# Tile homes moved to 96 bytes above a multiple of 128, and another order at the end of layer 0's output projection

## The chip, the cores and the metric

The kernel runs on one core of a Trainium2 chip. The metric is the time of one execution on the device in microseconds (us). The runs of the kernel before took 1118.15, 1120.03 and 1122.57 us; their median is 1120.03 us. The profile is of a further execution, which took 1121.99 us.

## The reference, cut to what matters

The program is a decoder trunk of two layers on 512 tokens of width 1024, all in float32. Each layer adds a mixer and then a SwiGLU feed-forward part to the residual stream.

```python
for layer in range(2):
    h = h + mixer(rms_norm(h, g), w_in, ..., w_out)      # even_mixer, then odd_mixer
    h = h + swiglu(rms_norm(h, ffn_g[layer]), w_gate, w_up, w_down)
return rms_norm(h, final_norm_g)

def even_mixer(h, w_in, sinks, conv_w, conv_b, ln_g, ln_b, w_out, pos):   # layer 0
    q, k, v, glu = split(h @ w_in)
    a = band_attention(rotary(q), rotary(k), v, 127, sinks)   # 8 heads, 2 key heads, window 128
    c = glu_a * sigmoid(glu_b)
    c = silu(layer_norm(causal_depthwise_conv(c, conv_w, conv_b), ln_g, ln_b))   # width 31
    return concat([a, c]) @ w_out
```

Layer 0's output projection reads eight tiles of 128 channels: four of attention, four of the convolution. Layer 1 mixes a dilated attention with a gated product; its arithmetic is not touched.

## The kernel before, in words

**Products.** Activations lie transposed: a tile has 128 channels as partitions and 512 tokens along them. A float32 product is done as three products of a faster type: each operand is split into a high part (ScalarE rounds it) and a low part (VectorE or GpSimd subtracts), and `acc3` (L197 on) multiplies high by high, high by low and low by high (L201 to L203), each a matmul of 512 columns. In the projections the weights (`w_hi`, `w_lo`) are the stationary operand and the activation streams. In the feed-forward part the first two products are done in seven block products (L909, L911, L912), where the weights (`w2h`, `w2l`) stream and the activations are stationary: `xh`, `xl` in three of the seven, sums `s1` to `s4` in four. The down product is again `acc3`, with the hidden tiles `hh`, `hl` streaming.

**Homes.** Every tile has a fixed address in each partition, handed out in the order of the calls, each rounded up to 32 bytes. The pools `const`, `keep`, `wpool` and `scr` stand for the whole kernel; a fourth region is used in turn by the pools of layer 0's mixer, of the feed-forward part and of layer 1's mixer. The build gives these homes (address modulo 512, and modulo 128):

| tiles | mod 512 | mod 128 |
|---|---|---|
| `ident` | 288 | 32 |
| `h`, `xh`, `xl`, `raw`, `w_hi`, `w_lo` | 352 | 96 |
| feed-forward: `w2h`, `w2l`, `raw2`, `hh`, `hl`, `s1` to `s4` | 288 | 32 |
| layer 1's mixer: `oh`, `ol`, `st` | 288 | 32 |
| layer 0's mixer: `oh`, `ol`, `yc`, `khh`, `qs` | 416 | 32 |

**Order.** TensorE runs its instructions in the order in which they are written out. A planner in the kernel (`Seq`) writes it: it keeps a clock of its own, adds 0.682 us for each `acc3` and lets generators step in when their due times have come: scores (`scores0`), values (`values0`, which calls `pt_av`) and the convolution's layer norm (`conv_norm`). The due times are the constants of `C0`. `until` jumps the clock to the next due time when a step needs a result that the plan has not reached. The other engines are ordered by the framework, each engine in order again.

In layer 0, `pt_av` transposes the softmax tiles in groups of four (L407), ScalarE copies each group out of PSUM (`pts`, L410), and TensorE multiplies it by the values (L421); VectorE normalises (`on`, L430), and TensorE transposes back (L435). `at[g]` is the planned time from which a group may be multiplied: 0.9 us after its transposes (`TA`).

The convolution runs beside this: `conv_tile` has 31 taps for each of four channel tiles, some on ScalarE with GpSimd (L478, L479), most on VectorE (L481, L483), and a last sum (L484). `conv_norm` transposes each finished channel tile (L645), gathers statistics (L647), and after the fourth forms the norm and transposes back (L672); a SiLU on ScalarE (L675) and a split give the tiles `L0` to `L3` that the projection needs.

The word list `steps` orders all this. `A0` to `A3` are the projection of attention tile 0 to 3 into the output tiles `na` = (0, 1), `X` the same into `nx` = (2, 3, 4), `Y` the four attention tiles into output 5, 6 or 7, and `B` one convolution tile into outputs 0 to 4. `C12` ends the list: for each of the outputs 0 to 4 the convolution tiles 1 and 2, and then the residual sum. Outputs 5 to 7 follow. The output tile `n` is summed in PSUM bank `n`; the last projection before `A0` (`q3`) has its result in bank 0, and `b3` had its own in bank 1.

Of the kernel before, what the change touches and what calls it, by code (L numbers as in the profile page):

```python
# [10 lines left out]
def _warn_once_fixed(msg, *args, **kwargs):  # L11
# [7 lines left out]
F32 = mybir.dt.float32  # L19
F32R = mybir.dt.float32r  # L20
AF = mybir.ActivationFunctionType
ALU = mybir.AluOpType

P = 128
S = 512
# [9 lines left out]
C0 = dict(  # L35

    first='a0 b0',
    steps='L g0 k q0 v S0 g1 q1 V0 S1 g2 q2 V1 S2 g3 q3 V2 S3 V3 A0 A1 A2 Y5 X0 X1 A3 Y6 X3 X2 Y7 B0 B3 C12',  # L40
    na=(0, 1), nx=(2, 3, 4),
    rope_v=('k', 'q2', 'q3'),
    taps=(8, 15, 15, 10),

    norm=(0.0, 2.6), q=(11.0, 7.0, 7.0, 6.0), v=1.2, S=3.13, ST=3.0, TA=0.9, AO=2.4, LB=4.85, LO=2.1, LS=3.5, ln=(60.0, 84.0, 112.0, 124.0),

    n1=5, q1=6.6, S1=2.26, ST1=3.65, m1=11.78, M1=0.53, TA1=1.12, AO1=1.4,
)
# [86 lines left out]
def trunk_kernel(ctx: ExitStack, tc: tile.TileContext, xT, ws, cols, sinks, sgu_g, sgu_b,  # L135
                 spat_wT, spat_b, rope_c, rope_s, ident_d, mask0_d, mask1_d, fin_g, y):
    nc = tc.nc
    V, A, G, T = nc.vector, nc.scalar, nc.gpsimd, nc.tensor
    ctx.enter_context(tc.manual_schedule(engines={mybir.EngineType.PE}))

    const = ctx.enter_context(tc.tile_pool(name="const", bufs=1))
    keep = ctx.enter_context(tc.tile_pool(name="keep", bufs=1))
    wpool = ctx.enter_context(tc.tile_pool(name="wpool", bufs=4))
    scr = ctx.enter_context(tc.tile_pool(name="scr", bufs=2))
    psum = ctx.enter_context(tc.tile_pool(name="psum", bufs=1, space=bass.MemoryType.PSUM))

    def bank(i, shape=None):
        return psum.tile(shape or [P, S], F32, name=f"bank{i}")
# [94 lines left out]
    seq = Seq()  # L243
# [47 lines left out]
    for k in range(2, KT):  # L291
        nc.sync.dma_start(h[k], xT[k])
        if k in (3, 6):
            dma_block()
    ident = const.tile([P, P], F32, name="ident")
    nc.sync.dma_start(ident, ident_d)
    ones = const.tile([P, 1], F32, name="ones")
    V.memset(ones, 1.0)
    mhalf = const.tile([P, 4], F32, name="mhalf")
    V.memset(mhalf, -0.5)  # L300

    idle = scr.tile([P, 256], F32, name="sq", bufs=1)
    V.memset(idle, 0.0)
# [10 lines left out]
    norm = {}  # L314
# [80 lines left out]
    def pt_av(items, vap, rl, dst, banks, line="V", ta="TA", ao="AO"):  # L395

        po = bank(5, [P, 8, 64])
        turn = [0]

        def tbank():  # L400
            turn[0] += 1
            return bank(banks[(turn[0] - 1) % len(banks)])

        def trans(grp):
            pt = tbank()
            for x, (u, pap, blk, first, last) in enumerate(grp):
                T.transpose(pt[:, x * P:(x + 1) * P], pap, ident)  # L407
            pts = mpool[0].tile([P, S], F32, name="pts", bufs=3)
            w = len(grp) * P
            A.activation(pts[:, :w], pt[:, :w], AF.Copy)  # L410
            return pts

        grps = [items[c:c + 4] for c in range(0, len(items), 4)]
        pts, at = {}, {}
        for g in range(min(2, len(grps))):
            pts[g] = trans(grps[g])
            at[g] = seq.t + 0.43 + C0[ta]
            yield 0.43, (0.0 if g == 0 else max(0.0, at[0] - seq.t - 0.43))
        for g, grp in enumerate(grps):
            for x, (u, pap, blk, first, last) in enumerate(grp):  # L420
                T.matmul(po[:, u, :], pts[g][:, x * P:(x + 1) * P], vap(u, blk), start=first, stop=last)  # L421
            cost = 0.43
            if g + 2 < len(grps):
                pts[g + 2] = trans(grps[g + 2])
                at[g + 2] = seq.t + 0.86 + C0[ta]
                cost = 0.86
            if g + 1 < len(grps):
                yield cost, max(0.0, at[g + 1] - seq.t - cost)
        on = mpool[0].tile([P, NQ, P], F32, name="on", bufs=1)
        V.tensor_mul(on.rearrange("p n (b e) -> p (n b) e", b=2), po,  # L430
                     rl[:, :, None].to_broadcast([P, 8, 64]))
        yield 0.43, C0[ao]
        pt = tbank()
        for n in range(NQ):
            T.transpose(pt[:, n * P:(n + 1) * P], on[:, n, :], ident)  # L435
        split(pt, oh_[0][dst], ol_[0][dst])
        done.add((line, dst))
        yield 0.43, 0.0
# [5 lines left out]
    with ExitStack() as mx:  # L444
        mp = mx.enter_context(tc.tile_pool(name="mix0", bufs=1))
# [5 lines left out]
        nc.sync.dma_start(sinkb, bass.AP(tensor=sinks.tensor, offset=sinks.offset, ap=[[0, P], [1, 8]]))  # L451
        nsink = mp.tile([P, 8], F32, name="nsink")
        V.tensor_scalar(out=nsink, in0=sinkb, scalar1=-1.0, scalar2=None, op0=ALU.mult)
        cp = [mp.tile([P, TAPS - 1 + S], F32, name=f"cp{j}") for j in range(4)]
        for j in range(4):
            G.memset(cp[j][:, 0:TAPS - 1], 0.0)
# [2 lines left out]
        V.tensor_scalar(out=taps, in0=taps, scalar1=0.5, scalar2=None, op0=ALU.mult)  # L459


        mp.tile([P, 8, 2 * P + 1], F32, name="Pm", bufs=2)
        for b in range(2):
            mp.tile([P, S], F32R, name=f"qs{b}", bufs=2)
        yc = [mp.tile([P, S], F32, name=f"yc{j}") for j in range(4)]
# [107 lines left out]
        def scores0(i):  # L573
            yield 0.0, C0["q"][i]
            while i >= 2 and ("V", i - 2) not in done:
                yield 0.0, 0.3
            qss = qTs[i]

            Pm = mp.tile([P, 8, 2 * P + 1], F32, name="Pm", bufs=2)
            A.activation(Pm[:, :, 2 * P:].rearrange("p (n b) o -> p n (b o)", b=2),  # L580
                         nsink[:, i:i + 5:4][:, None, :].to_broadcast([P, NQ, 2]), AF.Copy)
            nm = scr.tile([P, 8], F32, name="nm")
            l = scr.tile([P, 8], F32, name="l")
            for n2 in range(2):
                sb = [bank(2), bank(3)]
                for n1 in range(2):
                    n = 2 * n2 + n1
                    for b in range(2):
                        lo = max(n - 1, 0) * P
                        w = (n + 1) * P - lo  # L590
                        out = sb[b][:, n1 * 256 + 256 - w:n1 * 256 + 256]
                        q = slice(n * P, (n + 1) * P)
                        T.matmul(out, qss[b][:, q], khh[b][:, lo:lo + w], start=True, stop=False)
                        T.matmul(out, qss[b][:, q], kl[b][:, lo:lo + w], start=False, stop=True)
                for n1 in range(2):
                    n = 2 * n2 + n1
                    for b in range(2):
                        u = 2 * n + b
                        c0 = P if n == 0 else 0
                        hd = i + 4 * b  # L600
                        V.tensor_tensor_reduce(
                            out=Pm[:, u, c0:2 * P], in0=sb[b][:, n1 * 256 + c0:n1 * 256 + 256],
                            in1=mask0[:, c0:], scale=-0.125, scalar=nsink[:, hd:hd + 1],
                            op0=ALU.add, op1=ALU.min, accum_out=nm[:, u:u + 1])
                if n2 == 0:
                    yield 0.9, C0["S"]
            for u in range(8):
                c0 = P if u < 2 else 0
                A.activation(Pm[:, u, c0:], Pm[:, u, c0:], AF.Exp, bias=nm[:, u:u + 1], scale=-1.0,
                             accum_out=l[:, u:u + 1])  # L610
            rl = scr.tile([P, 8], F32, name="rl")
            V.reciprocal(rl, l)
            del qTs[i]
            pend[i] = Pm, rl, seq.t + 0.9 + C0["ST"]
            yield 0.9, 0.0
# [70 lines left out]
        for step in C0["steps"].split():  # L686
# [56 lines left out]
            else:  # L743
# [3 lines left out]
                k = i + 4 if kind == "B" else i  # L747
# [319 lines left out]
    with ExitStack() as mx:  # L1067
        mp = mx.enter_context(tc.tile_pool(name="mix1", bufs=1))
# [67 lines left out]
        def scores1(i, qk, ql):  # L1136
            yield 0.0, C0["q1"]
            while i >= 2 and ("V1", i - 2) not in done:
                yield 0.0, 0.3
            Pm = [mp.tile([P, 10 * P], F32, name="Pm", bufs=3) for _ in range(2)]  # L1140
            nm = scr.tile([P, 8], F32, name="nm")
            rl = scr.tile([P, 8], F32, name="rl")
            for n in range(NQ):
                w = (n + 1) * P
                q = slice(n * P, w)
                sb = [bank(2), bank(3)]
                for b in range(2):
                    qs, ks = qk[b]
                    T.matmul(sb[b][:, :w], qs[:, q], ks[:, :w], start=True, stop=False)
                    T.matmul(sb[b][:, :w], ql[b][:, q], ks[:, :w], start=False, stop=True)  # L1150
                for b in range(2):
                    u = 2 * n + b
                    V.tensor_tensor_reduce(
                        out=Pm[b][:, offs[n]:offs[n] + w], in0=sb[b][:, :w],
                        in1=mask1[:, S - w:], scale=-0.125, scalar=3.0e38,
                        op0=ALU.add, op1=ALU.min, accum_out=nm[:, u:u + 1])
                    A.activation(Pm[b][:, offs[n]:offs[n] + w], Pm[b][:, offs[n]:offs[n] + w], AF.Exp,
                                 bias=nm[:, u:u + 1], scale=-1.0, accum_out=rl[:, u:u + 1])
                if n < NQ - 1:
                    yield 0.22 * (n + 1), C0["S1"]  # L1160
            V.reciprocal(rl, rl)
            pend[i] = Pm, rl, seq.t + 0.9 + C0["ST1"]
            yield 0.9, 0.0
# [182 lines left out]
```

## Time and profile before

| what | value |
|---|---|
| median of three runs | 1120.03 us |
| the profiled execution | 1121.99 us |
| its span, first to last instruction | 1120.3 us |
| TensorE busy | 1082.4 us, 97% |
| VectorE busy | 692.2 us, 62% |
| ScalarE busy | 570.3 us, 51% |
| GpSimd busy | 233.3 us, 21% |
| mean granted TensorE clock | 0.990 |

The execution takes 1.69 us more than its span. The input projection and attention of layer 0 take the first 145 us, its output projection ends near 192 us, its feed-forward part near 546 us; layer 1's mixer ends near 753 us. Busy times of TensorE count a pipelined matmul (0.39 us) while the next one already runs, so the distance from one start to the next, about 0.23 us, is the better measure.

### The profile page before, as it was taken

The numbers are of one execution on the slowest core, as the hardware profiler recorded it, in microseconds if no ns is written. First come the engines' busy times: TensorE is split into PE (matmuls) and PEld (weight loads), VectorE is DVE, ScalarE is ACT, GpSimd is POOL, SyncE is SP. The second block draws the span as 40 slices with busy tenths as digits, with TensorE's granted clock in tenths as the row PEclk, the third lists the DMA queues.
The fourth block names the chain that finished last, engine by engine and source line by source line (L and its number), as shares of the span: only waits on it lengthen the run. The fifth ranks groups of instructions, "written<-read, shape, count | busy, mean of one in ns | idle before, by whom it ended". The sixth has DMA issues, their size and how long they took to land.

```text
span 1120.3 us, 13714 instructions
## 1 busy us (share of the span) xinstructions
PE 1082.4 (97%) x5118; PEld 888.2 (79%) x5118; DVE 692.2 (62%) x1051; ACT 570.3 (51%) x930; POOL 233.3 (21%) x210
## 2 busy tenths in 40 slices
PE   9989889999999999999999999999999999999997
PEld 7877767878878888888887888787778788888785
DVE  3889966866565556564647647556665645555543
ACT  6577745754444353533546654446544443535433
POOL 0889944211101010100023300002111010101002
PEclk9989999999999999999998999999999999999999
DMA  6211113977767676611521111239877676666122
GB/s 230 69 57 62 46 57 112 273 204 179 187 151 167 175 150 188 135 35 63 168 90 57 57 57 58 82 111 263 213 179 185 151 169 186 139 192 141 27 68 76
DMA packets 42803, 145.89 MB, mean 130 GB/s; under 512 B 4848, under 2 KB 5744, under 8 KB 42736
## 3 DMA queue, kind: packets, MB, share of 16 engines
q1 hardware_dynamic: 30496, 100.88, 26.2%
q0 software_dynamic: 11520, 41.95, 21.9%
q10 hardware_dynamic: 720, 2.18, 0.6%
q8 instruction: 40, 0.66, 0.2%
q14 instruction: 27, 0.22, 0.1%
HBM read 142.89 MB, written 2.10 MB: 129 GB/s over the span
## 4 chain that ended last, share of the span: by engine, by line
PE 75%; DVE 11%; DMA 5%; ACT 4%; issue 3%; POOL 1%; POOLq 0%; ACTq 0%; SPq 0%
PE bank L911 10%; PE bank L912 10%; PE bank L909 10%; PE bank L201 10%; PE bank L202 10%; PE bank L203 10%; DMA raw<-in_ws 5%; DVE bank L483 3%; PE bank L262 2%; PE bank L264 2%; PE bank L263 2%; PE bank L421 2%; PE bank L924 1%; DVE w2l L151 1%; ACT w2h L885 1%
## 5 line engine op out<-in xcount | busy, mean ns | idle before, releaser
L151 DVE TENSOR_TENSOR w2l<-raw,w2h 128x1024 fp32r<-128x1024 f32 x140 | 171.2, 1225 | 209.0 <-ACT w2h L885 208.8
L885 ACT ACTIVATE w2h<-raw 128x1024 fp32r<-128x1024 f32 x140 | 147.7, 1058 | 213.6 <-PE bank L912 161.2
L174 ACT ACTIVATE w_hi<-raw 128x512 fp32r<-128x512 f32 x204 | 127.7, 628 | 193.0 <-PE bank L202 153.4
L875 POOL DMA_DIRECT2D raw<-in_ws x80 | 69.5, 877 | 560.2 <-DVE w2l L151 235.3
L151 DVE TENSOR_TENSOR w_lo<-raw,w_hi 128x512 fp32r<-128x512 f32 x164 | 117.1, 717 | 58.6 <-ACT w_hi L174 56.5
L911 PE MATMUL bank<-w2l,s 128*128 128x512 f32 x320 | 125.3, 391 | 2.6 <-DVE w2l L151 2.5
L909 PE MATMUL bank<-w2h,s 128*128 128x512 f32 x320 | 125.6, 393 | 1.4 <-DVE gb L845 1.3
L912 PE MATMUL bank<-w2h,s 128*128 128x512 f32 x320 | 124.9, 390 | 0.0
L201 PE MATMUL bank<-xh,w_hi 128*128 128x512 f32 x272 | 110.8, 407 | 1.1 <-ACT w_hi L174 1.1
L203 PE MATMUL bank<-xh,w_lo 128*128 128x512 f32 x272 | 107.6, 396 | 0.0
L202 PE MATMUL bank<-xl,w_hi 128*128 128x512 f32 x272 | 107.2, 394 | 0.0
L201 PE MATMUL bank<-hh,w_hi 128*128 128x512 f32 x256 | 101.4, 396 | 0.0
L203 PE MATMUL bank<-hh,w_lo 128*128 128x512 f32 x256 | 101.2, 395 | 0.0
L202 PE MATMUL bank<-hl,w_hi 128*128 128x512 f32 x256 | 101.2, 395 | 0.0
L909 PE MATMUL bank<-w2h,xh 128*128 128x512 f32 x240 | 95.7, 399 | 0.0
L911 PE MATMUL bank<-w2l,xh 128*128 128x512 f32 x240 | 94.8, 395 | 0.0
L912 PE MATMUL bank<-w2h,xl 128*128 128x512 f32 x240 | 94.8, 395 | 0.0
L911 PEld LDWEIGHTS bank<-w2l,s 128*128 128x128 f32 x320 | 60.1, 188 | 16.7 <-DVE w2l L151 4.1
L909 PEld LDWEIGHTS bank<-w2h,s 128*128 128x128 f32 x320 | 60.1, 188 | 15.1 <-DVE gb L845 1.7
L912 PEld LDWEIGHTS bank<-w2h,s 128*128 128x128 f32 x320 | 60.1, 188 | 12.6
L151 POOL TENSOR_TENSOR w_lo<-raw,w_hi 128x512 fp32r<-128x512 f32 x40 | 54.5, 1364 | 64.7 <-ACT w_hi L174 61.9
L939 DVE TENSOR_TENSOR h<-h,bank 128x512 f32<-128x512 f32 x69 | 47.1, 685 | 26.1 <-PE bank L203 26.1
(235 smaller groups left out, 2067.8 us busy)
## 6 DMA issues: line engine op xcount, KB each, us to landing
raw<-in_ws SPq DMA_DIRECT2D x177, 512.0 KB, 4.3
raw<-in_ws POOLq DMA_DIRECT2D x80, 512.0 KB, 5.7
h<-in_xT SPq DMA_DIRECT2D x8, 256.0 KB, 5.0
raw<-in_ws ACTq DMA_DIRECT2D x4, 512.0 KB, 4.6
out_y<-xh SPq DMA_DIRECT2D x4, 256.0 KB, 2.0
out_y<-xl SPq DMA_DIRECT2D x4, 256.0 KB, 2.3
raw<-in_ws SPq DMA_DIRECT2D x2, 256.0 KB, 4.0
ropeC<-in_rope_c SPq DMA_DIRECT2D x2, 256.0 KB, 4.1
```

Of the source, the lines that this page charges most:

```text
L151: eng.tensor_tensor(out=out, in0=a, in1=b, op=ALU.subtract)
L174: A.activation(hi, src, AF.Copy)
L201: T.matmul(ps, hi, xh, start=start, stop=False)
L202: T.matmul(ps, hi, xl, start=False, stop=False)
L203: T.matmul(ps, lo, xh, start=False, stop=stop)
L483: V.scalar_tensor_tensor(acc, src, w, acc, op0=ALU.mult, op1=ALU.add)
L875: nc.gpsimd.dma_start(t, ws[base + 8 * (g - 1) + 2 * BLOCK_OF[more] + q], accum_op=ALU.add)
L885: A.activation(hi, src, AF.Copy)
L909: T.matmul(ps[t], xh[:, c], wh[:, w], start=(start and j == 0), stop=False, skip_group_check=True)
L911: T.matmul(ps[t], xh[:, c], wl[:, w], start=False, stop=False, skip_group_check=True)
L912: T.matmul(ps[t], xl[:, c], wh[:, w], start=False, stop=(j == 3), skip_group_check=True)
L939: V.tensor_add(h[n], h[n], ps)
```

## The change

Some tiles are moved or made larger, so that the homes after them shift: `ident` is taken after two small tiles, `rl` has 64 bytes in place of 32 (it has two buffers, so all after it lies 64 bytes higher), a tile `gap` of 64 bytes is added in layer 0's mixer, and the rows of `Pm` have 264 elements in place of 257. By the same arithmetic `ident`, the feed-forward tiles and layer 1's tiles then lie at 352 modulo 512 (96 modulo 128), and layer 0's `oh`, `ol`, `yc`, `khh` and `qs` at 480 modulo 512 (96 modulo 128). `h`, `xh`, `xl`, `raw`, `w_hi` and `w_lo` stay. The layer 0 planner gets `TF=1.6`, which is added to the due time of the first group of each `pt_av`; `na` is turned to (1, 0); and the end of `steps` is `B0 B1 C23` in place of `B0 B3 C12`. The host lays out the weights in the new order.

```diff
-    steps='... X2 Y7 B0 B3 C12',
-    na=(0, 1), nx=(2, 3, 4),
+    steps='... X2 Y7 B0 B1 C23',
+    na=(1, 0), nx=(2, 3, 4),
-    norm=(0.0, 2.6), ..., TA=0.9, AO=2.4, ...
+    norm=(0.0, 2.6), ..., TA=0.9, TF=1.6, AO=2.4, ...
-    ident = const.tile([P, P], F32, name="ident")
-    nc.sync.dma_start(ident, ident_d)
     ones = const.tile([P, 1], F32, name="ones")
     V.memset(ones, 1.0)
     mhalf = const.tile([P, 4], F32, name="mhalf")
     V.memset(mhalf, -0.5)
+    ident = const.tile([P, P], F32, name="ident")
+    nc.sync.dma_start(ident, ident_d)
...
-            at[g] = seq.t + 0.43 + C0[ta]
+            at[g] = seq.t + 0.43 + C0[ta] + (C0["TF"] if ta == "TA" and g == 0 else 0.0)
...
+        mp.tile([P, 16], F32, name="gap")
...
-            Pm = mp.tile([P, 8, 2 * P + 1], F32, name="Pm", bufs=2)
+            Pm = mp.tile([P, 8, 2 * P + 8], F32, name="Pm", bufs=2)
...
-                A.activation(Pm[:, u, c0:], Pm[:, u, c0:], AF.Exp, bias=nm[:, u:u + 1], scale=-1.0,
+                A.activation(Pm[:, u, c0:2 * P + 1], Pm[:, u, c0:2 * P + 1], AF.Exp, bias=nm[:, u:u + 1], scale=-1.0,
...
-            rl = scr.tile([P, 8], F32, name="rl")
+            rl = scr.tile([P, 16], F32, name="rl")[:, :8]
```

## Rows read from the trace of the kernel before

**Rows 1.** The page, parts 1 and 4: busy time by engine, and the chain.

```profile
PE 1082.4 (97%) x5118; PEld 888.2 (79%) x5118; DVE 692.2 (62%) x1051; ACT 570.3 (51%) x930; POOL 233.3 (21%) x210
...
PE 75%; DVE 11%; DMA 5%; ACT 4%; issue 3%; POOL 1%; POOLq 0%; ACTq 0%; SPq 0%
```

**Rows 2.** The page, part 5: groups; after the bar idle time and its releaser.

```profile
L885 ACT ACTIVATE w2h<-raw 128x1024 fp32r<-128x1024 f32 x140 | 147.7, 1058 | 213.6 <-PE bank L912 161.2
...
L201 PE MATMUL bank<-hh,w_hi 128*128 128x512 f32 x256 | 101.4, 396 | 0.0
...
L909 PE MATMUL bank<-w2h,xh 128*128 128x512 f32 x240 | 95.7, 399 | 0.0
```

**Rows 3.** Timeline of TensorE, layer 0's feed-forward part, homes 288 against 352: start, length.

```profile
309.12 0.40 PE L201 MATMUL bank<-hh,w_hi 128*128 128x512 f32 x1
...
331.29 0.40 PE L203 MATMUL bank<-hh,w_lo 128*128 128x512 f32 x1
```

**Rows 4.** Timeline of TensorE, two stretches with both operands' homes alike.

```profile
192.64 0.40 PE L201 MATMUL bank<-xh,w_hi 128*128 128x512 f32 x1
...
203.34 0.40 PE L203 MATMUL bank<-xh,w_lo 128*128 128x512 f32 x1
...
466.12 0.48 PE L909 MATMUL bank<-w2h,s 128*128 128x512 f32 x1
...
482.33 0.39 PE L912 MATMUL bank<-w2h,s 128*128 128x512 f32 x1
```

**Rows 5.** Timeline of TensorE, layer 1's output projection, homes 288 against 352.

```profile
708.78 0.50 PE L201 MATMUL bank<-oh,w_hi 128*128 128x512 f32 x1
...
752.75 0.39 PE L203 MATMUL bank<-st,w_lo 128*128 128x512 f32 x1
```

**Rows 6.** Timeline of TensorE, layer 0's output projection, homes 416 against 352.

```profile
146.34 0.39 PE L201 MATMUL bank<-oh,w_hi 128*128 128x512 f32 x1
...
155.03 0.39 PE L203 MATMUL bank<-oh,w_lo 128*128 128x512 f32 x1
```

**Rows 7.** Windows: stretch, busy time by engine, PEclk the granted clock, DMA.

```profile
28.00:119.40 91.40, 85.56 (x438) 72.06 (x436) 82.37 (x159) 66.56 (x141) 79.11 (x59) 0.96 0.20 66
119.40:155.30 35.90, 30.21 (x177) 25.72 (x177) 30.50 (x56) 20.77 (x46) 24.94 (x20) 0.95 0.11 32
...
210.00:560.00 350.00, 347.58 (x1544) 282.01 (x1543) 208.87 (x266) 158.93 (x218) 32.19 (x37) 1.00 0.62 155
...
68.10:74.90 6.80, 6.80 (x32) 6.51 (x32) 3.94 (x6) 4.78 (x10) 6.72 (x6) 0.50 0.15 58
122.70:126.10 3.40, 3.40 (x16) 3.11 (x15) 2.67 (x3) 2.17 (x4) 3.40 (x3) 0.50 0.48 159
```

**Rows 8.** Timeline of TensorE in layer 0; in brackets idle time before, and releaser.

```profile
67.83 0.48 PE L421 MATMUL bank<-Vt,pts 128*128 128x64 f32 x2 [2.03 <-ACT pts L410]
...
99.94 0.32 PE L421 MATMUL bank<-Vt,pts 128*128 128x64 f32 x1 [1.42 <-ACT pts L410]
...
121.44 0.47 PE L201 MATMUL bank<-oh,w_hi 128*128 128x512 f32 x1 [1.89 <-DVE rb L391]
...
155.26 0.38 PE L645 MATMUL bank<-ident,yc 128*128 128x128 f32 x2
...
166.53 0.50 PE L201 MATMUL bank<-oh,w_hi 128*128 128x512 f32 x1 [0.85 <-ACT oh L363]
...
173.49 0.49 PE L201 MATMUL bank<-oh,w_hi 128*128 128x512 f32 x1 [1.33 <-DVE oh L677]
```

**Rows 9.** VectorE: two rows of its timeline, two of its waits, 28 to 151.4 us.

```profile
150.61 0.69 DVE L484 TENSOR_TENSOR yc<-yc,bank 128x512 f32<-128x512 f32 x1
155.90 0.30 DVE L647 BATCH_NORM_STATS2 bs<-bank 128x6 f32<-128x128 f32 x1 [4.60 <-PE bank L645]
...
DVE qs L721 <- ACT qs L720: 2.8, 2, 2.1
DVE on L430 <- PE bank L421: 1.4, 1, 1.4
```

More of the change, by code (lines that the diff above doesn't have):

```diff
@@ L39 @@
     first='a0 b0',
-    steps='L g0 k q0 v S0 g1 q1 V0 S1 g2 q2 V1 S2 g3 q3 V2 S3 V3 A0 A1 A2 Y5 X0 X1 A3 Y6 X3 X2 Y7 B0 B3 C12',
-    na=(0, 1), nx=(2, 3, 4),
+    steps='L g0 k q0 v S0 g1 q1 V0 S1 g2 q2 V1 S2 g3 q3 V2 S3 V3 A0 A1 A2 Y5 X0 X1 A3 Y6 X3 X2 Y7 B0 B1 C23',
+    na=(1, 0), nx=(2, 3, 4),
     rope_v=('k', 'q2', 'q3'),
     taps=(8, 15, 15, 10),
-    norm=(0.0, 2.6), q=(11.0, 7.0, 7.0, 6.0), v=1.2, S=3.13, ST=3.0, TA=0.9, AO=2.4, LB=4.85, LO=2.1, LS=3.5, ln=(60.0, 84.0, 112.0, 124.0),
+    norm=(0.0, 2.6), q=(11.0, 7.0, 7.0, 6.0), v=1.2, S=3.13, ST=3.0, TA=0.9, TF=1.6, AO=2.4, LB=4.85, LO=2.1, LS=3.5, ln=(60.0, 84.0, 112.0, 124.0),
     n1=5, q1=6.6, S1=2.26, ST1=3.65, m1=11.78, M1=0.53, TA1=1.12, AO1=1.4,
@@ L459, in trunk_kernel @@
         V.tensor_scalar(out=taps, in0=taps, scalar1=0.5, scalar2=None, op0=ALU.mult)
-        mp.tile([P, 8, 2 * P + 1], F32, name="Pm", bufs=2)
+        mp.tile([P, 8, 2 * P + 8], F32, name="Pm", bufs=2)
         for b in range(2):
@@ L577, in scores0 @@
             qss = qTs[i]
-            Pm = mp.tile([P, 8, 2 * P + 1], F32, name="Pm", bufs=2)
-            A.activation(Pm[:, :, 2 * P:].rearrange("p (n b) o -> p n (b o)", b=2),
+            Pm = mp.tile([P, 8, 2 * P + 8], F32, name="Pm", bufs=2)
+            A.activation(Pm[:, :, 2 * P:2 * P + 1].rearrange("p (n b) o -> p n (b o)", b=2),
                          nsink[:, i:i + 5:4][:, None, :].to_broadcast([P, NQ, 2]), AF.Copy)
@@ L1141, in scores1 @@
             nm = scr.tile([P, 8], F32, name="nm")
-            rl = scr.tile([P, 8], F32, name="rl")
+            rl = scr.tile([P, 16], F32, name="rl")[:, :8]
             for n in range(NQ):
```

## The prediction

> **What bounds the kernel now.** I read the page first: TensorE is busy 97% of the span and makes up 75% of the chain that ended last [rows 1]. The reader is to see that no other engine passes 62%. Then the groups: ScalarE's `w2h` copies wait 161.2 us for TensorE to give buffers back, so in the feed-forward parts weights are made sooner than they are used [rows 2]. The windows show two kinds of stage. From 210 to 560 us TensorE is idle for 2.4 of 350 us: there the time is the number of matmuls times the distance from one start to the next. From 28 to 155.3 us VectorE is busy 112.9 of 127.3 us and TensorE idles 11.5 us in bits [rows 7]: layer 0's mixer is shared between TensorE and VectorE's convolution. So I took the start-to-start distance from the timeline, sorted by the homes of the two operands, and for layer 0 the single stalls.
>
> **Homes.** Where the streaming operand lies at 288 and the stationary one at 352 modulo 512, 96 matmuls of 512 columns (half `hh` against `w_hi`, half `w2h` against `xh`) take 22.17 us for 95 distances, 233.4 ns each [rows 3]; layer 1's output projection has 233.9 ns over 188 distances [rows 5]. Where both lie alike it is 227.7 ns (both at 352) and 228.3 ns (both at 288) [rows 4], none of the four with a stall inside, and the clock granted in full from 210 to 560 us [rows 7]. The kind of product isn't the reason: `w2h` as streaming operand is slow against `xh` and fast against `s`, and `w_hi` as stationary operand is slow under `hh` and fast under `xh`. What differs is the offset of the homes. I take 233.4 - 228.0 = 5.4 ns as its price, 228.0 being the middle of the two fast stretches. It is paid by 3 x 256 matmuls of the down products and 3 x 240 of the block products [rows 2], by 192 in layer 1's output projection (64 tiles of three; 189 of them in [rows 5]) and by 96 in layer 0's last down product (32 tiles, whose hidden tiles stand in `s1` and `s2`): 1776 in all. After the change both homes are 352 modulo 512 for each of them, and 1776 x 5.4 ns = 9.6 us goes. Nothing hides it: TensorE is the limit there, and if it gets 2% faster, ScalarE, which waits for its buffers, is not late next. The ends: 4.9 ns each by the slower fast stretch against 233.2 (8.7 us), 6.2 ns by the faster one against 233.9 (11.0 us), and 0 if the homes have nothing to do with it.
>
> Two further sets have no row for what they become. Layer 0's output projection goes from an offset of +64 to one of +128, which the trace does not show; now it takes 228.7 ns [rows 6]. Its 192 matmuls could go to 227.7 or to 233.9 [rows 4, 5]: between 0.2 us less and 1.0 more; I take 0, the value of the nearest row. Layer 1's very last product (192 matmuls, weights streaming) comes from +64 to 0: between 0 and 0.2 us less by [rows 6, 4]; I take 0.
>
> The Trainium skill speaks against this part: "SBUF — State Buffer", section "SBUF: two separate sides", says that TensorE, ScalarE and VectorE's own port pair wait on no one, and "TensorE: Matmul & The Clock Gate", section "Step-by-step: what each phase is for", gives TensorE two independent read ports, one for the streaming operand and one for the weights. By that rule the offset of two homes changes nothing and this term is 0; the trace does not agree, since 233.4 and 228 ns stand in one stage.
>
> **Edits that cost nothing.** The load of `ident` passes no other load on SyncE's queue, only two tiny fills on VectorE at the start, and it is needed first when the norm's scale is formed. `gap` is never written. `rl`, `nm` and the exponentials keep their element counts; the exponentials' slices of 257 elements already start at eight different offsets in `Pm`. Each I put at 0, with 0.1 us either way as I have no row of the new form.
>
> **The end of `steps` and `na`.** (a) In `B0 B3 C12` TensorE reaches `B3` before its tile is split and waits 1.33 us for VectorE at 173.49 us [rows 8]. With `B1` there, tile 1 was ready with tile 0 at 166.53, and `C2`, `C3` come after five more output tiles (15 x 0.229 = 3.4 us). The wait goes: -1.3 us; nothing new waits behind it. (b) `A0` now starts in bank 0, which VectorE's rope of `q3` still reads: 1.89 us at 121.44 us [rows 8]. Bank 1 had `b3`, whose gate VectorE is given before that rope. The second output of `A0` needs bank 0 only after the first one's three matmuls and eight transposes. So most of this wait goes, if VectorE stays where it is.
>
> **`TF`.** In the planner's arithmetic the first group of each `pt_av` comes 1.6 us later, which puts four tiles before the first product of `V0` and `V1`, and three before that of `V2`, where now stands one. This is no semaphore: two or three tiles of 0.69 us change places with the product. It covers the waits for `pts` of 2.03 us at 67.83 and of 1.42 us at 99.94 [rows 8]. After the first of these, TensorE's granted clock is 0.50 from 68.1 to 74.9 us, its level of 1.2 GHz; after the wait for bank 0 the same from 122.7 to 126.1 [rows 7]. Half of that time, 3.4 + 1.7 us, is lost work if the clock would else have stayed at 2.4 GHz. So up to 2.0 + 1.4 + 1.9 + 5.1 = 10.4 us of TensorE time comes free before 145 us. In `V3` no tile is left to fill; only the planner's clock jumps 1.7 us further. By it the fourth channel tile of the convolution, due at 124, is transposed two tiles (1.4 us) earlier in TensorE's order.
>
> **What is late next.** That transposition is the gate. It stands at 155.26, and the first `B` tile 11.27 us behind it [rows 8], a chain of statistics, norm, transposes and SiLU. VectorE writes the channel tile at 150.61 + 0.69 = 151.3 us, and its statistics then waited 4.60 us for TensorE [rows 9]. Before 151.3 VectorE has little idle time to give: 2.8 us for `qs` and 1.4 us for `on` [rows 9], the latter a wait for TensorE. So however much TensorE gains, the transposition comes at 151.4 us or up to 4.2 us before, and I take 151.4: -3.9 us. Of the 10.4 us the rest turns into waits for VectorE, in `A0`'s second output, in the scores `S3` and at this transposition. The 11.27 us behind it hold 11 tiles now and 13 then; 13 x 0.69 = 9.0 us still fits.
>
> **Sum.** Homes -9.6, gate -3.9, `B3` -1.3: -14.8 us. The profiled execution of 1121.99 us would become 1107.2. It stands 1.96 us above the median of the runs, so for the median I say 1120.0 - 14.8 = 1105.2 us.
>
> **Rivals.**
> 1. *Homes do nothing*, the slow rows having a reason that I don't see. For it: only a handful of offsets occur in the trace, and each belongs to a few lines. Against it: both orders of operands, the two layers and two kinds of product agree to 0.5 ns. Time: 1120.0 - 3.9 - 1.3 = 1114.8 us. This is also what the skill's rule gives.
> 2. *Layer 0 gives everything back.* VectorE and GpSimd are busy 113 and 104 of 127 us there [rows 7], in fixed order; if their order is drawn up anew around TensorE's and the last convolution sum ends at 156 instead of 151.3, the gate is no earlier, and the bit saved at `B3` goes too. Against it: four waits of TensorE vanish by construction, and the gate has 3.9 us of room. Time: 1120.0 - 9.6 = 1110.4 us, less what is kept of the waits.
> 3. *Slower: alike is worse when all is alike.* Now the writers in the feed-forward part (`w2h`, `w2l` at 288) lie off the home of `xh` at 352; then ScalarE, VectorE and TensorE all work at 352. If a read is held up by writes at the same offset, the 5.4 ns would fall on all 4144 matmuls of 512 columns: 1776 already pay it, 2368 would begin to, +12.8 us. Less 5.2 us in layer 0 this is 1127.6 us; it decides from about 1000 matmuls on (5.4 us against 5.2). Against it: the block products with `s` run at 228.3 ns while their writers lie at the same 288, and the gate and up projections at 227.7 ns with all at 352 [rows 4].
>
> **Chances.** Forecast 0.66, rival 2 0.18, rival 1 0.10, rival 3 0.06. The forecast alone spans 1099 to 1109: below, the homes at 11.0 us and VectorE 4.2 us earlier (20.4 us in all); above, 8.7 us of homes, 1.3 at `B3` and a quarter of the gate's gain. The range that holds 8 in 10 takes in rival 2 and most of what lies between it and rival 1: 1098 to 1114. A difference of 0.5%, 5.6 us, is about what a measurement tells from none. Below 1114.4 lie the forecast, rival 2 and nearly half of rival 1: faster 0.88. Same: the rest of rival 1 and little of the others, 0.07. Slower: most of rival 3, 0.05.
>
> **What would show it.** In the profile after: the down and block products at 228 ns from start to start throughout, and about 0.9 us less for each feed-forward group (168 of its matmuls pay now: 3 x 24 in block products, 96 in the down product); no wait for `pts` near 67 and 100 us and full clock behind it; no wait at the second `B` tile; the last channel transposition near 151 us, waiting for VectorE. I am wrong on the homes if equal homes still show 233 ns; wrong on layer 0 if the first `B` tile starts later than 164 us.

## Result and profile after

The changed kernel takes 1104.97 us (median of 4 runs, 1102.27 to 1106.53) against 1121.30 us before on the same chip (4 runs: the three given above and one more, of 1123.71): ratio 0.9853, 95% interval 0.982 to 0.9887. Forecast was 1105.2, range 1098 to 1114. The profiled execution took 1104.72 us (span 1103.0), 17.3 us less than the one profiled before.

The page of the changed kernel: busy time by engine, the shares of the chain, and three groups (busy, mean ns | idle before, releaser).

```profile
PE 1071.7 (97%) x5118; PEld 889.7 (81%) x5118; DVE 690.9 (63%) x1051; ACT 570.2 (52%) x930; POOL 234.6 (21%) x210
...
PE 77%; DVE 9%; ACT 4%; DMA 4%; issue 3%; POOL 2%; POOLq 0%; ACTq 0%; DVEq 0%
...
L886 ACT ACTIVATE w2h<-raw 128x1024 fp32r<-128x1024 f32 x140 | 147.8, 1059 | 210.4 <-PE bank L913 157.8
...
L201 PE MATMUL bank<-hh,w_hi 128*128 128x512 f32 x256 | 99.8, 390 | 0.0
...
L910 PE MATMUL bank<-w2h,xh 128*128 128x512 f32 x240 | 94.4, 393 | 0.0
```

The same 5118 matmuls are busy 10.7 us less, the other engines do what they did within 1.3 us, and TensorE has a larger share of the chain than in [rows 1]. The mean of one down or block product is only 6 ns shorter than in [rows 2], since a pipelined matmul counts until its end.

The distance between starts says it directly. The timeline of TensorE in the changed kernel (start, length): the down product that answers to [rows 3], layer 0's output projection behind its second convolution tile, which answers to [rows 6], and layer 1's, which answers to [rows 5].

```profile
303.94 0.39 PE L201 MATMUL bank<-hh,w_hi 128*128 128x512 f32 x1
...
325.47 0.39 PE L203 MATMUL bank<-hh,w_lo 128*128 128x512 f32 x1
...
168.16 0.48 PE L201 MATMUL bank<-oh,w_hi 128*128 128x512 f32 x1
...
188.30 0.40 PE L203 MATMUL bank<-oh,w_lo 128*128 128x512 f32 x1
...
697.52 0.50 PE L201 MATMUL bank<-oh,w_hi 128*128 128x512 f32 x1
...
740.27 0.39 PE L203 MATMUL bank<-st,w_lo 128*128 128x512 f32 x1
```

The down product: 95 distances in 21.53 us, 226.6 ns (233.4 in [rows 3]). Layer 1's output projection: 188 distances, 227.4 ns (233.9 in [rows 5]). Layer 0's output projection, now at +128: 86 distances, 234.2 ns (228.7 at +64 in [rows 6]). So the price has gone where it was expected to go, and has come up where I took 0.

Windows of layer 0 (busy time by engine; the last three columns are the granted clock, the DMA share and GB/s). The stretches from 28 and from 119.4 us answer to [rows 7].

```profile
7.80:11.00 3.20, 3.20 (x8) 2.53 (x9) 2.53 (x4) 3.20 (x7) 0.00 (x0) 0.50 1.04 401
28.00:119.40 91.40, 88.60 (x457) 74.57 (x455) 82.09 (x162) 67.16 (x143) 81.03 (x60) 0.96 0.21 70
76.00:82.80 6.80, 6.21 (x20) 5.34 (x21) 6.17 (x15) 3.81 (x11) 6.57 (x5) 0.50 0.21 77
119.40:155.30 35.90, 31.45 (x168) 26.61 (x169) 30.07 (x59) 19.92 (x46) 24.57 (x19) 0.86 0.10 34
127.20:137.40 10.20, 9.43 (x36) 7.78 (x35) 9.77 (x25) 6.49 (x16) 9.51 (x9) 0.50 0.00 0
```

The half clock (0.50 granted, TensorE's level of 1.2 GHz) of [rows 7] near 68 and 122 us has not vanished. It stands at 76.0 (6.8 us) and 127.2 (10.2 us), and once more at 7.7 (3.4 us). This last one puts everything behind it 1.7 us late (by the first transposition of `ga`, 45.28 us before, 47.00 now); some of the kernels below have it, others not, whatever was edited.

TensorE's timeline in layer 0 (in brackets the wait before and its releaser) and VectorE's at the gate, which answer to [rows 8] and [rows 9]; the row at 153.64 is the last channel transposition, and 165.70 the first `B` tile.

```profile
74.91 0.33 PE L594 MATMUL bank<-khh,qs 128*128 128x128 f32 x1 [1.18 <-DVE qs L722]
...
76.59 0.48 PE L594 MATMUL bank<-khh,qs 128*128 128x128 f32 x1 [1.24 <-DVE qs L722]
...
119.79 0.50 PE L201 MATMUL bank<-oh,w_hi 128*128 128x512 f32 x1 [0.43 <-DVE rb L391]
...
126.03 1.79 PE L421 MATMUL bank<-Vt,pts 128*128 128x64 f32 x12 [1.53 <-ACT pts L410]
...
153.64 0.60 PE L646 MATMUL bank<-ident,yc 128*128 128x128 f32 x4
...
165.70 0.39 PE L201 MATMUL bank<-oh,w_hi 128*128 128x512 f32 x1
```

```profile
151.05 0.69 DVE L485 TENSOR_TENSOR yc<-yc,bank 128x512 f32<-128x512 f32 x1
154.28 0.89 DVE L648 BATCH_NORM_STATS2 bs<-bank 128x6 f32<-128x128 f32 x4 [2.54 <-PE bank L646]
```

The waits near 67 and 100 us are gone. Waits for `qs` have grown (1.5 us in all before, 2.4 now), and at 126.03 one of 1.53 us for `pts` is new: it stands before the third group of `V2`. Before the change one output tile stood ahead of that group and one behind it; `TF` has put both ahead of the first group, so nothing is left there to cover the copy. In the view of TensorE's waits from 28 to 200 us the named waits add up to 15.5 us before and 7.7 after. The convolution's last channel tile is ready at 151.74, yet TensorE transposes it only at 153.64, in its own order: the gate is still TensorE's.

Where the 17.3 us went, by the start of the same instruction in both traces: end of layer 0's output projection 192.41 to 188.30, 4.1 us less (5.8 without the late start); feed-forward part of layer 0, 5.5; layer 1's mixer, 2.9; last feed-forward part, 4.9. In layer 1's mixer 192 matmuls give some 1.2 us, and a half-clock stretch that was 6.8 us long near 590 is 3.4 near 581, worth 1.7 us. That one looks like chance: the kernels below have it at 3.4 us or not at all, whatever was edited, each with the same wait of 2.6 to 2.7 us for `st` beside it.

### The profile page after: what moved, and what is told of

Same layout as the page of the kernel before. It is cut to its first block, busy times and chain, and to the rows that moved or that the text cites. A ratio compares the mean times of both kernels' runs of the same rounds, so it can differ in the third digit from the quotient of the medians.

```text
span 1103.0 us, 13715 instructions
## 1 busy us (share of the span) xinstructions
PE 1071.7 (97%) x5118; PEld 889.7 (81%) x5118; DVE 690.9 (63%) x1051; ACT 570.2 (52%) x930; POOL 234.6 (21%) x210
## 4 chain that ended last, share of the span: by engine, by line
PE 77%; DVE 9%; ACT 4%; DMA 4%; issue 3%; POOL 2%; POOLq 0%; ACTq 0%; DVEq 0%
PE bank L912 10%; PE bank L913 10%; PE bank L910 10%; PE bank L201 10%; PE bank L202 10%; PE bank L203 10%; DMA raw<-in_ws 4%; PE bank L262 2%; PE bank L264 2%; PE bank L263 2%; DVE bank L484 2%; PE bank L421 2%; PE bank L925 1%; DVE w2l L151 1%; PE bank L407 1%
## 5 line engine op out<-in xcount | busy, mean ns | idle before, releaser
L886 ACT ACTIVATE w2h<-raw 128x1024 fp32r<-128x1024 f32 x140 | 147.8, 1059 | 210.4 <-PE bank L913 157.8
L201 PEld LDWEIGHTS bank<-xh,w_hi 128*128 128x128 f32 x272 | 52.6, 193 | 12.3 <-ACT w_hi L174 2.2
```

The costliest lines, as they stand in the source:

```text
L201: T.matmul(ps, hi, xh, start=start, stop=False)
L886: A.activation(hi, src, AF.Copy)
```

## Experiments

Ratios are to the kernel before, run beside each on the same chip, with 95% intervals. "Net of the start" takes off by how much the first transposition of `ga` stands later than in the kernel before: 1.4 to 1.7 us where a profile shows TensorE at half clock near 7 us, 0.1 to 0.3 us elsewhere.

**Homes and order by themselves.** The first kernel has all homes of the change and the old order; the second the new order and the old homes.

```diff
# homes alone: the changed kernel with
+    steps='... B0 B3 C12', na=(0, 1), norm=(... TF=0.0 ...)
# order alone: the kernel before with
+    steps='... B0 B1 C23', na=(1, 0), norm=(... TF=1.6 ...)   # and TF's term in pt_av
```

> The moved homes alone, with the old order of layer 0 (TF 0, na (0, 1), B0 B3 C12). Theory (the price sits in the offset between the home of the streaming and that of the stationary operand): every down and block product at 227 to 228 ns from start to start, and the time 9 to 12 us below the kernel before, about two thirds of the whole change. Rival (the homes matter only together with the new order, or do nothing): at most 3 us below.

> The new order of layer 0 alone (TF 1.6, na (1, 0), B0 B1 C23), all homes as before. Theory: layer 0 ends 3 to 6 us earlier, the down products stay at 233 ns, the time 3 to 6 us below the kernel before. Rival (VectorE's convolution takes it all back): within 1 us of the kernel before.

Homes alone: 1111.23 us against 1121.44, 0.9899 [0.9877, 0.9921], by the ratio 11.3 us less (8.9 to 13.8; by the medians 10.2). Order alone: 1113.76, 0.9935 [0.9914, 0.9956], 7.3 us less (4.9 to 9.6). Both parts work without the other, and the two together come to about the whole (18.6 against 16.5, intervals of over 2 us on each). The down product that answers to [rows 3], first with homes alone, then with the order alone:

```profile
313.62 0.39 PE L201 MATMUL bank<-hh,w_hi 128*128 128x512 f32 x1
...
335.15 0.39 PE L203 MATMUL bank<-hh,w_lo 128*128 128x512 f32 x1
```

```profile
303.81 0.40 PE L201 MATMUL bank<-hh,w_hi 128*128 128x512 f32 x1
...
325.98 0.40 PE L203 MATMUL bank<-hh,w_lo 128*128 128x512 f32 x1
```

95 distances each: 226.6 ns with the new homes, 233.4 with the old.

**The homes themselves, or their distance?** All tiles 32 bytes higher, so that the pairs are alike but no longer 96 above a multiple of 128; and, in the old order, homes shifted so that the old pairs stand at +64, or at +256, in place of -64.

```diff
# all up: the changed kernel with
+    const.tile([P, 8], F32, name="pad0")      # ahead of ident
# +64 and +256: the kernel before with
+            rl = scr.tile([P, 24], F32, name="rl")[:, :8]      # 48 for +256
```

> The changed kernel with every home but the first tile's 32 bytes higher, so the homes are alike but at 0 above a multiple of 128 and not at 96. Theory (only the offset between two operands counts): down and block products stay at 227 to 228 ns and the time is that of the changed kernel, about 16 us below the kernel before. Rival (96 above a multiple of 128 is itself the good home): 233 ns somewhere and at least 5 us of the gain lost.

> The kernel before with the feed-forward and mixer homes 128 bytes higher, so they lie 64 above those of xh and w_hi modulo 512 where they lay 64 below; modulo 128 nothing changes, 32 against 96. Theory (the price depends on the signed offset, as the trace of before has 229 ns where the streaming operand lies 64 above): the down products go to 229 ns, while the block products with xh go there too, and the time falls by 5 to 8 us. Rival (only homes modulo 128 count): 233 ns stay, and the time stays within 1 us of the kernel before.

> The kernel before, order untouched, with the feed-forward and mixer homes 320 bytes higher, so that they lie 256 above those of xh and w_hi modulo 512 (32 against 96 becomes 96 against 96 modulo 128). Theory 1 (the offset counts modulo 256): down and block products at 227 to 228 ns, the time as with the moved homes alone, about 1110 us. Theory 2 (it counts modulo 512 or more): another figure, between 229 and 236 ns, and 1115 us or more.

All up: 1102.33 us, 0.9821 [0.9805, 0.9838], no slower than the change. Its down product takes 226.6 ns a matmul too:

```profile
301.83 0.39 PE L201 MATMUL bank<-hh,w_hi 128*128 128x512 f32 x1
...
323.36 0.39 PE L203 MATMUL bank<-hh,w_lo 128*128 128x512 f32 x1
```

What counts is where one home stands against the other, and 96 has no part in it. At +64: 1115.32, 0.9949 [0.993, 0.9969]; at +256: 1108.73, 0.9883 [0.9862, 0.9905]. The homes modulo 128 are the same pair (32 and 96) at -64 and at +64, and the time isn't: modulo 128 is not the rule. The down product answering to [rows 3], first the kernel at +64, then the one at +256:

```profile
307.70 0.39 PE L201 MATMUL bank<-hh,w_hi 128*128 128x512 f32 x1
...
329.45 0.39 PE L203 MATMUL bank<-hh,w_lo 128*128 128x512 f32 x1
```

```profile
308.71 0.39 PE L201 MATMUL bank<-hh,w_hi 128*128 128x512 f32 x1
...
330.24 0.39 PE L203 MATMUL bank<-hh,w_lo 128*128 128x512 f32 x1
```

95 distances each: 228.9 ns at +64, 226.6 at +256, as when alike. The table gathers, over these traces, the mean distance of 512-column matmuls at full clock by where the streaming home stands against the stationary one (neighbours with the same offset and no wait between them; the few distances of 260 ns and more are left out).

| streaming home less stationary home, modulo 256 | ns from start to start (matmuls, kernel) |
|---|---|
| 0 | 227.2 (3758, changed); 226.9 (1897, as +256 in the one at +256); 228.1 (1807, before) |
| +64 | 229.0 (350, before); 229.0 (1709, at +64) |
| +128 | 232.9 (171, changed); 232.6 (165, as +384 in the one at +256) |
| +192 | 233.4 (1713, as -64 in the kernel before); 233.3 (164, as +192 in the one at +64) |

These are means: at +64 single distances run from 226 to 232 ns, at +192 from 230 to 236. Only multiples of 64 occur. Which two accesses meet is not shown: the profile counts the loads of the next weights (PEld) as busy 81% of the span beside TensorE's 97%, and in these streams the weights loaded next nearly always lie at the same home modulo 256 as those in use.

**Layer 0's output projection at +128.** The filler `gap` becomes 448 bytes long, which brings layer 0's large tiles to 352 modulo 512 too. The second kernel has the old `na` besides.

```diff
-        mp.tile([P, 16], F32, name="gap")
+        mp.tile([P, 112], F32, name="gap")
```

> The changed kernel with a gap of 448 in place of 64 bytes, so that layer 0's oh, ol and yc lie at 352 modulo 512 like w_hi, where the change left them 128 above. Theory (the price depends on the offset; 128 costs 5 to 6 ns a matmul in the changed trace): layer 0's output projection goes from 232.9 to 227 to 228 ns, 192 matmuls, 0.5 to 1.1 us less. Rival (those few matmuls are slow for another reason, the writes beside them): no difference.

> The changed kernel with layer 0's oh, ol and yc at the home offset of w_hi (gap of 448 bytes) and na back at (0, 1): the two variations that were no slower than the changed kernel together. Theory (na is worth nothing with VectorE as the limit, the offset about 1 us): 1102 to 1104 us. Rival (noise): 1105 us.

1104.76 us, 0.9851 [0.9835, 0.9867], and 1105.17, 0.9852 [0.9831, 0.9873]: neither differs from the change. Its matmuls do run at 227.2 ns, and from the first `yc` product to the end of the projection it takes 21.81 us in place of 22.37 in the profiles. That is below what the runs can tell apart.

**`TF`.** Out altogether; only in `V0` and `V1`; out, with the fourth channel tile due at 122.3 in place of 124, so that its transposition moves up without it.

```diff
# out:                 norm=(... TF=0.0 ...)
# in V0 and V1 alone:  (C0["TF"] if ta == "TA" and g == 0 and dst < 2 else 0.0)
# out, tile due early: norm=(... TF=0.0 ...), ln=(60.0, 84.0, 112.0, 122.3)
```

> The changed kernel with TF taken back to 0; homes, na and the end of steps as changed. Theory (TF covers the copies of the first groups and draws the last channel transposition two tiles earlier): the waits for pts of about 2.2 us near 66 us and 1.6 us near 97 us are back, the last channel transposition 1.5 to 4 us later, the time 1.5 to 4 us above the changed kernel, about 12 to 15 us below the kernel before. Rival (VectorE's convolution sets the gate whatever TensorE does): within 1 us of the changed kernel.

> The changed kernel with TF for the values V0 and V1 alone; V2 and V3 as before, so the last channel transposition stands two tiles later, where it was without TF. Theory: the waits for pts at 67 and 97 us are covered, the rest not: 1107 to 1109 us. Rival A (TF is worth what it covers there): 1104 to 1106. Rival B (it is all the gate): 1111 to 1112. TF in V2 leaves TensorE short of tiles between 119 and 140 us, so a better time than the changed kernel is possible, with a shorter stretch at half clock there.

> The changed kernel with TF at 0 and the due time of the last channel transposition 122.3 in place of 124.0, which puts it in TensorE's order where the change has it (before the 20th output tile, two earlier than without TF). Theory (a good part of what TF is worth is the earlier gate, the rest the covered waits for pts): half of the way between the changed kernel without TF (1111.7 us) and the changed one, 1107 to 1109 us. Rival A (TF is worth what it covers at 67 and 97 us): no better than without TF, 1111 to 1112. Rival B (it is all the gate): 1104 to 1106.

Out: 1111.69 us, 0.9918 [0.9904, 0.9933], 6.7 us above the change, more than expected. `V0` and `V1` alone: 1106.09, 0.985 [0.9827, 0.9874], as good as the change as far as runs tell. Tile due early without `TF`: 1109.08, 0.9872 [0.9843, 0.99], runs from 1102.3 to 1111.8, which settles nothing. The edit did move the order (13 output tiles stand behind the gate, and the first `B` tile waits for nothing), yet in its profile the gate was no earlier (158.54): TensorE had 13.6 us at half clock ahead of it, from 133.5 and from 140.3. TensorE's timeline without `TF` shows what it covers:

```profile
69.57 0.66 PE L421 MATMUL bank<-Vt,pts 128*128 128x64 f32 x4 [2.04 <-ACT pts L410]
...
99.09 1.93 PE L421 MATMUL bank<-Vt,pts 128*128 128x64 f32 x12 [1.42 <-ACT pts L410]
...
168.39 0.49 PE L201 MATMUL bank<-oh,w_hi 128*128 128x512 f32 x1 [0.82 <-ACT oh L363]
169.67 0.50 PE L202 MATMUL bank<-yc,w_hi 128*128 128x512 f32 x1 [0.78 <-DVE yc L364]
```

The waits of [rows 8] for `pts` are back at their old size, and so are those at the first `B` tile. The gate stands at 157.14 (1.9 us later than in the kernel before, 0.2 net of the start), and VectorE waits there for TensorE:

```profile
157.78 0.89 DVE L648 BATCH_NORM_STATS2 bs<-bank 128x6 f32<-128x128 f32 x4 [6.61 <-PE bank L646]
```

So most of the order's gain comes from filling TensorE's waits in `V0` and `V1`. By the profiles the output projection ends 4.1 us earlier than before net of the start with `TF` there alone, against 5.8 with it everywhere; a rest of up to 1.7 us for `V2` and `V3` is below what these runs tell apart.

**`na` and the end of `steps`.** The changed kernel with each of them as it was.

```diff
# first:   na=(0, 1)
# second:  steps='... B0 B3 C12'
```

> The changed kernel with na back at (0, 1), so that the output projection begins in bank 0. Theory (bank 0 is still read by the rope of q3, but VectorE is the limit there): the wait of 1.9 to 3 us at the first output tile is back, most of it is lost anyway before the scores, and the time is 0 to 1.5 us above the changed kernel. Rival (every wait of TensorE counts in full): 2 us or more above.

> The changed kernel with the old end of steps, B0 B3 C12. Theory: the wait for the split of tile 3 is back at the second B step, 1.3 to 2.0 us in all, and the time 1.3 to 2.0 us above the changed kernel. Rival (the wait moves elsewhere, since tiles 2 and 3 at the end wait as well): no difference.

Old `na`: 1103.86 us, 0.9847 [0.983, 0.9865]: its turn is worth nothing that these runs can tell, though the wait at bank 0 is back:

```profile
118.07 0.57 PE L201 MATMUL bank<-oh,w_hi 128*128 128x512 f32 x1 [2.13 <-DVE rb L391]
```

Most of what the wait takes is given back later: it is 1.7 us longer than in the change, and the end of the output projection comes 5.2 us earlier than before net of the start, against 5.8 in the change. Old `steps`: 1106.61, 0.9871 [0.9846, 0.9897], not told apart from the change by its runs, which fall into two groups (1103.0 to 1103.6, and 1109.7 to 1111.0). Its profile, from the second group, shows the wait at the second `B` step back and one in the feed-forward part that no part of the change touches. TensorE, then ScalarE:

```profile
171.45 0.50 PE L202 MATMUL bank<-yc,w_hi 128*128 128x512 f32 x1 [1.22 <-DVE yc L679]
...
279.36 0.47 PE L201 MATMUL bank<-hh,w_hi 128*128 128x512 f32 x1 [1.61 <-DVE hl L151]
```

```profile
276.29 1.06 ACT L886 ACTIVATE w2h<-raw 128x1024 fp32r<-128x1024 f32 x1 [4.23 <-DMA raw<-in_ws]
```

ScalarE waits for a weight block that lands late; the `hh` copies stand behind it in its order, `hl` behind them, and TensorE waits 1.61 us. From 280.1 to 283.5 the granted clock is 0.50. The profiles of homes alone (1.58 us at 284.36) and of `TF` in `V0` and `V1` (1.88 us at 278.21) have the same wait and a half-clock stretch behind it; the changed kernel's has neither. This is one source of the spread of runs of one kernel; why the block is late in some runs only was not tried.

## Why the prediction was right, and where its steps were not

**Homes: right in place, too small by the distances.** The forecast's 9.6 us lies within the runs' 8.9 to 13.8, so the runs do not tell it from a larger figure. By the distances it is more. The 1776 matmuls that were to gain went from 233.3 to 226.9 ns (means over 1740 distances in each trace), which is 11.4 us: the price of 5.4 ns was too small, since 228.0, taken from pairs alike in the kernel before, was not where they ended. Those pairs that were alike all along went from 228.1 to 227.4 ns, on 1984 matmuls 1.2 us that I did not have. Layer 1's last product, from +64 to 0, gives 0.4; layer 0's output projection at +128 costs 192 x (232.9 - 229.0) = 0.7 where I took 0, inside the bound of 1.0. Together 12.3. Per feed-forward group it is 62.3 us in place of 63.4, 1.1 for the 0.9 forecast. Why pairs alike all along gain is open. It is mostly the block products with `s`: 227.9 ns in the two kernels where the pairs with `xh` beside them stand at -64, 226.9 to 227.1 with homes alone, with all up, at +64, at +256 and in the changed kernel.

**Rivals 1 and 3 fall with it.** The rule of the Trainium skill ("SBUF — State Buffer", "SBUF: two separate sides": TensorE's reads wait on no one) would make homes worth nothing. Homes alone gave 11.3 us, so the measurement decides against it here. And with nearly all pairs alike none of the alike ones is at 233 ns, where rival 3 had all of them.

**The gate: step wrong, sum about right.** "I take 151.4: -3.9 us" rested on VectorE's being late next. It wasn't. The transposition came at 153.64, 1.6 us earlier (3.3 net of the start), with its tile ready for 1.9 us; in the kernel with all homes up the tile is ready at 148.69 and the transposition stands at 150.60, again 1.9 us later. So VectorE's 151.3, read in the trace of before, was no floor either (the forecast had allowed for 4.2 us less), and in both kernels the order of TensorE's own work set the gate. By the prediction's own sign, a first `B` tile later than 164 us, layer 0 came out wrong: the tile starts at 165.70, and only net of the start at 164.0.

**The clock: step wrong.** "Full clock behind it" did not come. TensorE had 17.0 us at half clock from 28 us to the gate where it had 10.2, after shorter waits (1.18 and 1.24 us near 76; 1.53 us at 126). That takes back up to 6.8 / 2 = 3.4 of the 7.8 us of waits that went. The prediction counted what the moved tiles cover in `V0` and `V1`, and not what they leave uncovered in `V2`: the wait of 1.53 us at 126 is new, and the longer of the two stretches follows it.

**The tail: 2.5 us net, not 1.3.** `B3`'s wait went, as forecast. I counted that 11 tiles behind the gate become 13, and only asked whether they fit. They also fill the waits of 0.85 and 0.8 us at the first `B` tile: six matmuls fewer stand behind it, 1.4 us. That part belongs to `TF`: with it in `V0` and `V1` alone 11 tiles stand there and the waits are back (0.84 and 0.77 us). With the old `steps` the projection ends 4.0 us earlier than before net of the start, with the new 5.8: 1.8 us for this edit by the profiles.

**Order in sum.** Forecast 5.2, alone 7.3 (4.9 to 9.6). `TF` is nearly all of it. The bit for `na`, "most of this wait goes", was right as a wait and worth nothing in time. That layer 0 would give all back (rival 2) is refuted by the order alone.

**"ScalarE is not late next"** holds for the mean: its copies still wait 157.8 us for TensorE's buffers. In the first feed-forward group it fails in some runs, through a late weight block, for 1.6 to 1.9 us and a half-clock stretch.

**The hit to 0.2 us is partly luck.** By medians beside each other the gain is 16.3 us where the sum said 14.8; one more run of the kernel before raised its median by 1.3 us over the one that the forecast started from. And errors of both signs met: 2.7 us too little for the homes (by the distances) and 1.2 for the tail, against 1.7 us of late start and 0.6 too much at the gate (3.3 net in place of 3.9). The half clock that was not foreseen need not show in this sum: the forecast had put down 6.5 of its 10.4 us as lost to waits for VectorE, and in place of such waits up to 8.5 us (half of the 17.0) went to the clock.

## What to carry to other kernels

Take the distance from start to start of equal matmuls, sort it by where the two operands lie in SBUF relative to each other, and try a filler tile before anything cleverer: here a shift of 64 bytes was worth 1%. This is shown for 512-column matmuls in dense streams; other shapes were not measured. Where an engine in fixed order waits for a product's last input, move independent tiles in front of that product; and ask not only whether they fit, but how much of another wait they fill and which wait they leave open where they stood. The time at which another engine is ready, read in the old trace, is no floor for the new one.

## What the hardware showed that I had not expected

The pace of 512-column matmuls depends on the signed distance of the two homes modulo 256: 227 ns at 0, 229 at +64, 233 at +128 and at +192. -64 and +64 are not the same, and +256 is as good as 0. Other distances than multiples of 64 were not tried.

The granted clock went to 0.50 behind waits of 1.2 to 2 us in layer 0, and the place and length of such stretches changed between kernels that differ in homes alone (68.1 and 122.7 us before; 77.9, 234.9 and 286.1 in the kernel with homes alone). The one at 234.9 stands behind two waits of 0.8 us. Not every such wait is followed by one: the wait of 2.04 us at 69.57 without `TF` is not; there the next stretch begins at 100.1. And the wait of 2.6 us for `st` near 590 us has 6.8 us at half clock beside it in the kernel before, 3.4 in the changed one, and none with homes alone.
